# Dealing the projection steps of a two-layer hybrid block by kind of stage

## The chip, the cores and the metric

The kernel runs on one core of one Trainium2 chip. The metric is the device time of one execution in microseconds (us). The core's engines run side by side: TensorE (PE, matrix products), VectorE (DVE), ScalarE (ACT), GpSimd (POOL), and SyncE (SP), which here only issues DMAs.

## The reference

Two layers run over 256 context and 256 latent tokens of width 1024. In each layer one input projection feeds three mixers, and what this change touches is the first two lines and the scan:

```python
att, rw, cv, gt = split(h @ w_in, GROUP_SPLITS)       # h: modulated RMSNorm of the tokens
r, k, v, g, decay, k_dir, kk, a = rwkv_prepare(rw)    # token shift, low-rank decay, norms
# RWKV-7, both directions, 8 heads of 64, context first, then latents from its state:
state = state * w_t + (state @ a_t) b_t^T + v_t k_t^T ;  y_t = state @ r_t
o_rwkv = readout(y, r, k, v, g)                       # group norm, bonus, gate
o_att  = attention(att)                               # 8 query, 2 key heads, rotary
o_conv = b * conv3(c * u)                             # from cv
y = (sum_i sigmoid(gt_i) * (o_i @ w_br_i)) @ w_out    # three branches
x = x + g1 * y ;  x = x + g2 * expert_choice_ffn(...) # 16 experts, latents and context apart
```

In the second layer the context needs only what the latents read of it. Everything is in float32; the projections are split into a high and a low part and take three products.

## The kernel before, in words

Each layer runs in this order: the input norm, a loop over the RWKV scan, attention, the merge of the branches and the output projection (lines 1080 to 1240), and the experts (from line 1290 on), 16 of them with three matrices of 4 MB each to be streamed.

The scan is cut into chunks of 64 tokens and into four groups of two heads, `tau` = 0 to 3. The generator `stages(tau)` yields after each of its stages. Its first 29 are counted by `nx` = 0 to 28: the projections of k, r and v (`shifted`, matmuls into `ps_mm`), decay and step size, the key norm (L479, L484), the decays' scans and the scaled keys (DVE work, L505 to L525), the bonus (L532), the products within a chunk (L552), and the inverse of a unit triangular matrix per chunk. Its 16x16 blocks are inverted by a substitution on DVE (L575, L577); then two rounds of merges join the blocks to 32 and to 64, in the last five of the 29 stages: L591, L595, L609 and L616 are their tiny matmuls, 32x16 or 32x32, and between one and the next ACT and DVE copy, add and transpose (L592 to L619). Four more stages (v transposed at L633, the keys at L645, local products at L657, an empty one) and then eleven follow: the recurrence over eight chunks, with L671, L677 and L685 (`ps_ch`) and short DVE and ACT work in a ring, the output (L703, L707), its group norm (L717 to L729) and its gate (L736). The stages of `tau` + 1 are dealt between the recurrence steps of `tau`, some three at a time.

Filling work comes from the generator `fgen`: the projections of q, k and v of attention, of the convolution, and of 24 branch gates, 360 draws in all (a gate's ninth only closes it), into `ps_mf`. **A step** is one of eight slices of a projection's depth: three matmuls of 512 columns in layer 0 (L116 to L118) and, in layer 1, three of 256 columns (six where the context is needed too; L337). Every fourth step also takes a weight tile: one 256 KB DMA issued on SP (L356), a split into its high part on ACT (L102) and its low part on DVE (L103; three in four or two in three on POOL once attention has begun). After a gate's eighth step come a tanh on ACT (L762) and a DMA on ACT's queue.

`run(g, n, f)` advances a stage generator by n stages and after each of them owes `f` further steps; whole ones are drawn by `fill`. In layer 0 the loop over `tau` is followed by a top-up until 12 of the 24 gates are done (`GB`); in layer 1 the top-up asks for 8, which the loop has passed. The rest is drawn after attention in the text (with some loads of expert weights in between), and the compiler's list scheduler places it among attention's instructions. That scheduler orders each engine's instructions by their place in the text and by when they can be ready, so a step can move ahead of its place, as far as its two `ps_mf` buffers and its weight tiles allow.

Other matmuls in the loop are those of the modulation weights (L200, into `ps_mf` too).

## Time and profile before

| | us |
|---|---|
| median of 3 runs (2316.28 to 2330.32) | 2320.55 |
| profiled execution | 2315.12 |
| its span | 2313.3 |
| busy PE, DVE, ACT, POOL | 2015.0, 990.5, 703.5, 204.0 |
| mean granted TensorE clock | 0.910 of full |

The profiled execution is 1.8 us longer than its span and 5.43 us shorter than the median. Times inside the trace count from the span's start. Layer 0's loop lies from about 45 to 531, its attention to about 640, its experts to about 1269; layer 1's loop from 1278 to 1676, its attention to 1769, its experts from about 1850 to the end. A matmul's duration overlaps the next one's, so the pitch from start to start is what counts in a series of them; a matmul's end is modelled. Granted clock 1.00 is 2.4 GHz, and 0.50 is 1.2 GHz; a mean between them says how much of a stretch ran at which. In a table of stretches the busy times are those of PE, PE's weight loads, DVE, ACT and POOL, and the last three columns are the granted clock, the mean busy share of the 16 DMA engines and GB/s.

### The profile page before, as it was taken

The numbers are of one execution on the slowest core, as the hardware profiler recorded it, in microseconds if no ns is written. First come the engines' busy times: TensorE is split into PE (matmuls) and PEld (weight loads), VectorE is DVE, ScalarE is ACT, GpSimd is POOL, SyncE is SP. The second block draws the span as 40 slices with busy tenths as digits, with TensorE's granted clock in tenths as the row PEclk, the third lists the DMA queues.
The fourth block names the chain that finished last, engine by engine and source line by source line (L and its number), as shares of the span: only waits on it lengthen the run. The fifth ranks groups of instructions, "written<-read, shape, count | busy, mean of one in ns | idle before, by whom it ended". The sixth has DMA issues, their size and how long they took to land.

```text
span 2313.3 us, 44242 instructions
## 1 busy us (share of the span) xinstructions
PE 2015.0 (87%) x18191; PEld 1300.2 (56%) x18191; DVE 990.5 (43%) x2529; ACT 703.5 (30%) x1485; POOL 204.0 (9%) x221
## 2 busy tenths in 40 slices
PE   7999999998999899999987999997878887676765
PEld 3766676676688733333222987886767743232222
DVE  5767667535746511110102759667467511000001
ACT  3443434324523421212002644452354321010001
POOL 1000000003124300000000200000052300000000
PEclk7999999899999999999999989997899997676767
DMA  7333334454278779999999334334376999999997
GB/s 278 111 115 103 119 106 129 126 167 128 60 250 274 256 302 417 419 420 419 420 420 368 93 99 141 111 116 128 117 226 207 305 363 416 416 417 417 417 417 304
DMA packets 340445, 585.08 MB, mean 253 GB/s; under 512 B 20886, under 2 KB 203924, under 8 KB 339988
## 3 DMA queue, kind: packets, MB, share of 16 engines
q1 hardware_dynamic: 326846, 567.76, 67.1%
q10 hardware_dynamic: 13398, 14.50, 1.8%
q8 instruction: 143, 2.34, 0.4%
q14 instruction: 58, 0.48, 0.1%
HBM read 562.79 MB, written 19.40 MB: 252 GB/s over the span
## 4 chain that ended last, share of the span: by engine, by line
PE 41%; DMA 23%; DVE 6%; ACT 2%; issue 2%; POOL 1%; SPq 0%; DVEq 0%; ACTq 0%; POOLq 0%
PE ps_mf L1325 9%; DMA we<-in_exp_down_dram 9%; DMA we<-in_exp_up_dram 6%; DMA we<-in_exp_gate_dram 5%; PE ps_mm L1343 4%; PE ps_mf L337 4%; PE ps_mf L118 2%; PE ps_mf L116 2%; PE ps_mf L117 2%; PE ps_mm L337 2%; PE ps_ch L1167 2%; PE ps_ch L1355 1%; PE ps_sm L552 1%; PE ps_sm L1021 1%; PE ps_sm L1355 1%
## 5 line engine op out<-in xcount | busy, mean ns | idle before, releaser
L1325 PE MATMUL ps_mf<-we,xe 128*32 128x256 f32 (+1 forms) x3040 | 419.2, 534 | 88.0 <-DMA we<-in_exp_up_dram 47.1
L1325 PEld LDWEIGHTS ps_mf<-we,xe 128*32 128x32 f32 (+1 forms) x3040 | 137.2, 134 | 332.8 <-issue 150.2
L1343 PE MATMUL ps_mm<-we,hT 128*32 128x256 f32 (+1 forms) x1536 | 204.3, 526 | 43.2 <-DMA we<-in_exp_down_dram 29.8
L102 ACT ACTIVATE whi<-w 128x512 fp32r<-128x512 f32 x236 | 147.0, 629 | 240.0 <-PE ps_mf L117 73.6
L1330 DVE TENSOR_TENSOR hid<-hid,ps_mf 128x512 f32<-128x512 f32 (+1 forms) x32 | 17.7, 554 | 436.7 <-PE ps_mf L1325 436.0
L103 DVE TENSOR_TENSOR wlo<-w,whi 128x512 fp32r<-128x512 f32 x199 | 137.0, 693 | 81.4 <-ACT whi L102 27.0
L1343 PEld LDWEIGHTS ps_mm<-we,hT 128*32 128x32 f32 (+1 forms) x1536 | 68.4, 133 | 161.7 <-issue 70.7
L337 PE MATMUL ps_mf<-hT,whi 128*128 128x256 f32 x736 | 150.1, 298 | 3.0 <-ACT whi L102 2.8
L116 PE MATMUL ps_mf<-hhi,whi 128*128 128x512 f32 x344 | 143.8, 418 | 1.3 <-ACT csb L779 1.0
L118 PE MATMUL ps_mf<-hhi,wlo 128*128 128x512 f32 x344 | 140.7, 409 | 0.4 <-DVE wlo L103 0.4
L117 PE MATMUL ps_mf<-hlo,whi 128*128 128x512 f32 x344 | 140.4, 408 | 0.0
L1349 DVE TENSOR_TENSOR yg<-ps_mm,g2p 128x512 f32<-128x512 f32 (+1 forms) x32 | 17.9, 558 | 275.2 <-PE ps_mm L1343 275.2
L337 PEld LDWEIGHTS ps_mf<-hT,whi 128*128 128x128 f32 x736 | 117.9, 196 | 14.0 <-issue 4.7
L337 PE MATMUL ps_mf<-hT,wlo 128*128 128x256 f32 x368 | 106.0, 299 | 8.3 <-DVE wlo L103 5.1
L1353 ACT COPY ye<-yg 32x512 f32<-32x512 f32 (+1 forms) x64 | 32.6, 509 | 222.1 <-DVE yg L1349 220.2
L1335 ACT ACTIVATE hT<-ps_sm 128x512 f32<-128x512 f32 (+1 forms) x32 | 15.7, 490 | 235.1 <-PE ps_sm L1334 235.1
L337 PEld LDWEIGHTS ps_mf<-hT,wlo 128*128 128x128 f32 x368 | 70.7, 197 | 14.5 <-DVE wlo L103 5.9
L116 PEld LDWEIGHTS ps_mf<-hhi,whi 128*128 128x128 f32 x344 | 66.0, 192 | 21.4 <-issue 3.9
L118 PEld LDWEIGHTS ps_mf<-hhi,wlo 128*128 128x128 f32 x344 | 66.3, 193 | 16.3 <-issue 1.9
L117 PEld LDWEIGHTS ps_mf<-hlo,whi 128*128 128x128 f32 x344 | 66.1, 192 | 14.7 <-issue 2.6
L337 PE MATMUL ps_mm<-hT,whi 128*128 128x256 f32 x368 | 69.5, 303 | 4.0 <-DVE X L577 2.6
L1173 ACT ACTIVATE xe<-ps_ch,mod,A 128x128 f32<-128x128 f32 x84 | 38.1, 458 | 100.7 <-PE ps_ch L1167 100.6
(476 smaller groups left out, 3775.2 us busy)
## 6 DMA issues: line engine op xcount, KB each, us to landing
we<-in_exp_down_dram SPq DMA_DIRECT2D x124, 1024.0 KB
we<-in_exp_gate_dram SPq DMA_DIRECT2D x118, 1024.0 KB
we<-in_exp_up_dram SPq DMA_DIRECT2D x117, 1024.0 KB
w<-in_w_in_dram SPq DMA_DIRECT2D x228, 256.0 KB
adaw<-in_ada_w_dram SPq DMA_DIRECT2D x160, 256.0 KB
we<-in_exp_gate_dram SPq DMA_DIRECT2D x40, 256.0 KB
adaw<-in_ada_w_dram SPq DMA_DIRECT2D x16, 512.0 KB
cw<-in_w_out_dram SPq DMA_DIRECT2D x32, 256.0 KB
```

Source lines behind the costliest of these rows:

```text
L102: S.activation(hi, src, AF.Copy)
L103: (eng or G).tensor_tensor(lo, src, hi.bitcast(F32), op=ALU.subtract)
L116: P.matmul(o, lh[0], rh[0], start=first, stop=False)
L117: P.matmul(o, lh[0], rh[1], start=False, stop=False)
L118: P.matmul(o, lh[1], rh[0], start=False, stop=last)
L337: P.matmul(o[:, 256 * s - c0:256 * s - c0 + 256], w_[:, j], hT[s][x][:, k], start=first and i == 0 and 256 * s == c0, stop=last and i == 2 ...
L1167: P.matmul(pg, htok[si][:, t, j * 128:(j + 1) * 128], oh[:, t].rearrange("p e c -> p (e c)"), start=(t == 0), stop=(t == 1))
L1173: S.activation(dst, pge, AF.Identity, scale=A2[l][:, j, st_:st_ + 1], bias=mod[l][:, 24 + j, st_:st_ + 1])
L1325: P.matmul(pp[M * g:M * g + M], xe[e // 4][:, j, e % 4], w[:, jj, g * FW:(g + 1) * FW], start=(j == 0), stop=(j == 7), skip_group_check=True)
L1343: P.matmul(pd[M * g:M * g + M], hT2[:, q, M * fg:M * fg + M], w[:, jj, g * FW:(g + 1) * FW], start=(j == 0), stop=(j == 7), skip_group_che ...
L1353: (S.copy, V.tensor_copy)[(g + si) % 2](ye[32 * eg:32 * eg + 32, si, g * FW:(g + 1) * FW], yg[p0:p0 + 32])
L1355: return P.matmul(po, Pw[e // 4][:, tt // 2, (tt % 2) * 128:(tt % 2) * 128 + 128], ye[:, tt // 2, 512 * hf:512 * hf + 512], start=start, s ...
```

## The change

The four numbers per layer in `FR` get new meanings and values. Before, they were steps per stage for `nx` below 12, for the other stages up to 28, for the four stages behind them, and for the eleven of the recurrence and readout (`FL` for `tau` 3). Now they are steps per stage for `nx` below 24, for the merges (`nx` 24 to 28) and the four stages behind them together, for the eleven, and for the eleven of `tau` 3.

```diff
@@ -232,8 +232,7 @@
     SPF = (1, 1)
     SPC = (4, 3)
     GB = (12, 8)
-    FR = ([1.0, 1.0, 1.0, 1.0], [1.2, 1.2, 1.2, 1.2])
-    FL = (1.0, 4.0)
+    FR = ([0.85, 2.0, 1.0, 3.0], [0.95, 3.0, 1.0, 4.0])
     CW = (4, 5)
     CH = (3, 4)
     TH = (2, 3)
@@ -814,22 +813,24 @@
                     fill(f)
                 return True
 
-            FP, FI, FM, FC = FR[l]
+            FP, FM, FC, FL = FR[l]
+            many = lambda nx: FP if nx < 24 else FM
             sg_ = [stages(tau) for tau in range(4)]
             rows1 = vec_rows(1, pw, nc.sync) if l == 0 else None
             run(sg_[0], 12, FP)
             ny = 29
             if l == 0:
                 vec_cols(1, rows1)
-            run(sg_[0], ny - 12, FI)
+            for nx in range(12, ny):
+                run(sg_[0], 1, many(nx))
             for tau in range(4):
                 run(sg_[tau], 4, FM)
                 nx = 0
                 for s in range(11):
-                    run(sg_[tau], 1, FC if tau < 3 else FL[l])
+                    run(sg_[tau], 1, FC if tau < 3 else FL)
                     if tau < 3:
                         for _ in range(ny * min(s + 1, 10) // 10 - nx):
-                            run(sg_[tau + 1], 1, FP if nx < 12 else FI)
+                            run(sg_[tau + 1], 1, many(nx))
                             nx += 1
             while gdone[0] < GB[l] and next(fg, 0) != 0:
                 pass
```

Over a loop, 176 steps become 219.6 in layer 0 and 242 become 276.2 in layer 1. In layer 0 the top-up to 12 gates stays, so the steps done ahead of attention stay the same in number, and it has fewer to do. In layer 1 more steps are done in the loop, and fewer are left for attention.

Three places in PE's order follow. `ps_mf` rows of L116 to L118 or L337 are filling steps; lines of the change are lower by one. First, the merges of `tau` 3 in layer 0, before:

```order
L591 MATMUL ps_sm<-XT,Ad 32x16 x64
L724 MATMUL ps_ch<-ck,yq 128x2 x4
L116 MATMUL ps_mf<-hhi,whi 128x512
L117 MATMUL ps_mf<-hlo,whi 128x512
L595 MATMUL ps_sm<-Xd,Wm 32x16 x64
L118 MATMUL ps_mf<-hhi,wlo 128x512
L729 MATMUL ps_ch<-ck,rq_y 64x128 x8
L116 MATMUL ps_mf<-hhi,whi 128x512
L609 MATMUL ps_sm<-XT,Aa 32x32 x32
```

and now, to the second merge of the same place:

```order
L590 MATMUL ps_sm<-XT,Ad 32x16 x64
L116 MATMUL ps_mf<-hhi,whi 128x512
L117 MATMUL ps_mf<-hlo,whi 128x512
L118 MATMUL ps_mf<-hhi,wlo 128x512
L116 MATMUL ps_mf<-hhi,whi 128x512
L117 MATMUL ps_mf<-hlo,whi 128x512
L118 MATMUL ps_mf<-hhi,wlo 128x512
L716 MATMUL ps_ch<-y,cr 128x512
L594 MATMUL ps_sm<-Xd,Wm 32x16 x64
L723 MATMUL ps_ch<-ck,yq 128x2 x4
```

Between L591 and L595 there were two filling matmuls, and between L595 and L609 two; now there are six ahead of L594 (L595 before), and six follow up to L608.

The same merges in layer 1, before:

```order
L591 MATMUL ps_sm<-XT,Ad 32x16 x64
L729 MATMUL ps_ch<-ck,rq_y 64x128 x4
L595 MATMUL ps_sm<-Xd,Wm 32x16 x64
L736 MATMUL ps_ch<-gl,g2t 128x256
L609 MATMUL ps_sm<-XT,Aa 32x32 x32
L616 MATMUL ps_sm<-Xd,W2T 32x32 x32
```

and now, from L591's place (L590) on:

```order
L590 MATMUL ps_sm<-XT,Ad 32x16 x64
L336 MATMUL ps_mf<-hT,whi 128x256
L336 MATMUL ps_mf<-hT,wlo 128x256
L336 MATMUL ps_mf<-hT,whi 128x256 x2
L594 MATMUL ps_sm<-Xd,Wm 32x16 x64
L728 MATMUL ps_ch<-ck,rq_y 64x128 x4
L735 MATMUL ps_ch<-gl,g2t 128x256
L336 MATMUL ps_mf<-hT,wlo 128x256
L336 MATMUL ps_mf<-hT,whi 128x256 x2
L336 MATMUL ps_mf<-hT,wlo 128x256
L336 MATMUL ps_mf<-hT,whi 128x256 x2
L336 MATMUL ps_mf<-hT,wlo 128x256
```

No filling matmul stood among these merges, and now four stand behind the first and seven ahead of the third.

Last, attention's scores (L1010), transposes (L1021) and products (L1023) in layer 1, before:

```order
L1010 MATMUL ps_ch<-kT,qT 128x512 x2
L337 MATMUL ps_mf<-hT,wlo 128x256
L337 MATMUL ps_mf<-hT,whi 128x256
L1021 MATMUL ps_sm<-ck,pe 128x128 x4
L1010 MATMUL ps_ch<-kT,qT 128x512 x2
L337 MATMUL ps_mf<-hT,whi 128x256
L337 MATMUL ps_mf<-hT,wlo 128x256
L337 MATMUL ps_mf<-hT,whi 128x256 x2
L337 MATMUL ps_mf<-hT,wlo 128x256
L337 MATMUL ps_mf<-hT,whi 128x256 x2
L1021 MATMUL ps_sm<-ck,pe 128x128 x4
```

and now:

```order
L1011 MATMUL ps_ch<-kT,qT 128x512 x6
L1022 MATMUL ps_sm<-ck,pe 128x128 x4
L1011 MATMUL ps_ch<-kT,qT 128x512 x2
L1022 MATMUL ps_sm<-ck,pe 128x128 x4
L1011 MATMUL ps_ch<-kT,qT 128x512 x2
L1022 MATMUL ps_sm<-ck,pe 128x128 x4
L1011 MATMUL ps_ch<-kT,qT 128x512 x2
L1022 MATMUL ps_sm<-ck,pe 128x128 x4
L1011 MATMUL ps_ch<-kT,qT 128x512 x2
L1024 MATMUL ps_mm<-PT,qkv_16919 64x256 x4
L1024 MATMUL ps_mm<-PT,qkv_16920 64x256 x4
```

The filling matmuls, 92 from the first score on, are gone from here.

## Rows read from the trace of the kernel before

**Rows 1.** Page, part 2: the granted clock in 40 slices of 57.8 us.

```profile
PEclk7999999899999999999999989997899997676767
```

**Rows 2.** Stretches of layer 0: length, busy us (instructions) per engine, granted clock, DMA.

```profile
105.00:129.00 24.00, 22.37 (x133) 18.60 (x132) 20.97 (x67) 6.86 (x11) 0.31 (x1) 1.00 0.23 67
149.50:159.70 10.20, 10.20 (x103) 5.74 (x97) 6.46 (x17) 7.92 (x14) 0.00 (x0) 1.00 0.48 140
159.70:213.80 54.10, 49.07 (x498) 33.67 (x496) 44.77 (x134) 15.70 (x32) 1.90 (x6) 0.94 0.48 145
213.80:235.50 21.70, 21.50 (x553) 17.01 (x553) 11.24 (x31) 11.51 (x22) 0.00 (x0) 1.00 0.17 55
264.30:315.50 51.20, 46.05 (x491) 31.84 (x489) 43.75 (x132) 13.23 (x27) 1.89 (x6) 0.93 0.46 140
315.50:337.30 21.80, 21.78 (x554) 17.46 (x554) 12.99 (x34) 12.61 (x24) 0.11 (x1) 1.00 0.14 42
367.20:420.10 52.90, 49.60 (x494) 33.65 (x490) 44.83 (x133) 14.87 (x31) 0.75 (x3) 1.00 0.44 131
420.10:444.60 24.50, 24.22 (x545) 18.52 (x545) 10.17 (x29) 11.27 (x22) 0.00 (x0) 0.79 0.16 49
444.60:488.60 44.00, 39.22 (x470) 24.79 (x470) 19.82 (x67) 6.90 (x16) 0.00 (x0) 0.92 0.52 159
488.60:531.40 42.80, 42.54 (x186) 34.53 (x185) 14.02 (x21) 17.16 (x31) 6.88 (x5) 1.00 0.65 203
```

**Rows 3.** Stretches of layer 1, same columns.

```profile
1356.60:1377.30 20.70, 19.14 (x524) 17.81 (x526) 6.52 (x14) 10.73 (x21) 0.00 (x0) 0.75 0.15 42
1442.50:1462.00 19.50, 17.57 (x534) 16.20 (x536) 8.38 (x19) 9.78 (x19) 0.00 (x0) 0.82 0.25 74
1472.60:1524.20 51.60, 48.94 (x556) 41.87 (x554) 46.44 (x154) 19.50 (x41) 1.89 (x6) 1.00 0.49 145
1524.20:1546.90 22.70, 21.48 (x549) 19.99 (x547) 10.09 (x21) 12.23 (x24) 0.00 (x0) 0.77 0.17 51
1555.60:1610.70 55.10, 45.32 (x464) 36.55 (x465) 41.59 (x134) 16.25 (x36) 0.76 (x3) 0.81 0.48 150
1610.70:1631.80 21.10, 16.99 (x504) 14.95 (x506) 7.12 (x22) 9.12 (x18) 0.00 (x0) 0.60 0.13 38
1675.90:1729.20 53.30, 38.70 (x267) 35.08 (x265) 35.09 (x57) 26.11 (x61) 25.25 (x25) 0.94 0.75 225
1729.20:1768.70 39.50, 34.93 (x254) 28.21 (x252) 29.89 (x75) 22.54 (x54) 8.95 (x7) 1.00 0.60 184
1850.00:1860.00 10.00, 8.26 (x60) 5.47 (x61) 3.58 (x11) 1.72 (x4) 1.54 (x2) 0.63 0.39 130
1860.00:2300.00 440.00, 318.12 (x3222) 128.20 (x3220) 33.29 (x82) 39.66 (x95) 1.23 (x2) 0.73 1.01 412
```

**Rows 4.** Timeline of PE in layer 0: start, duration, engine, instruction, count.

```profile
163.74 0.39 PE L116 MATMUL ps_mf<-hhi,whi 128*128 128x512 f32 x1
163.97 0.40 PE L117 MATMUL ps_mf<-hlo,whi 128*128 128x512 f32 x1
```

**Rows 5.** Timeline of PE in layer 1, same columns.

```profile
1753.24 0.28 PE L337 MATMUL ps_mf<-hT,wlo 128*128 128x256 f32 x1
1753.36 0.40 PE L337 MATMUL ps_mf<-hT,whi 128*128 128x256 f32 x2
```

**Rows 6.** Waits from 1610 to 1632: total us, times, longest.

```profile
PE ps_sm L616 <- DVE W2T L612: 1.5, 1, 1.5
PE ps_sm L609 <- DVE XT L598: 1.2, 1, 1.2
```

**Rows 7.** Page, part 5: the splits' low part: count, busy us, mean ns, idle before.

```profile
L103 DVE TENSOR_TENSOR wlo<-w,whi 128x512 fp32r<-128x512 f32 x199 | 137.0, 693 | 81.4 <-ACT whi L102 27.0
```

**Rows 8.** Groups by line on PE in layer 1's attention, 1729.2 to 1768.7: filling matmuls.

```profile
L337 PE MATMUL ps_mf<-hT,whi 128*128 128x256 f32 x62 | 12.9, 286 | 0.0
L337 PE MATMUL ps_mf<-hT,wlo 128*128 128x256 f32 x32 | 9.2, 288 | 0.3 <-POOL wlo L103 0.3
```

## The prediction

> **What bounds the kernel now.** I read the page's clock line first, then tables of stretches for both loops, then PE's timeline for pitches, and the waits at one place. The clock line [rows 1] is at 9 or more through most of both loops and at 6 to 7 in the last stretch, layer 1's experts. Those run at 412 GB/s with the DMA engines full [rows 3]: they are bound by transfers, and nothing in them changes. Ten microseconds ahead of them the DMA share is only 0.39 [rows 3], so their prefetch is done by then: the stretch starts and ends earlier or later by whatever the loops and attention ahead of it gain or lose.
>
> The two loops have a rhythm. I call the part of a `tau` from its key norm (L479) to the first merge (L591) its **preparation**, from there to its first recurrence matmul its **merges**, and from there to the next key norm its **gap**. In layer 0 the preparations of `tau` 1 to 3 take 54.1, 51.2 and 52.9 us, with DVE busy 44.8, 43.8 and 44.8 and PE 49.1, 46.1 and 49.6 [rows 2]: both are nearly full. The merges take 21.7, 21.8 and 24.5 with PE full and DVE half idle [rows 2]. So steps compete with DVE's share of a preparation, and lengthen merges that PE already fills. Layer 0's loop has little empty PE time: about 5, 5 and 3 us per preparation and 4.8 in `tau` 3's recurrence and readout (44.0 less 39.2) [rows 2]. Layer 1 has more: in `tau` 3's preparation 9.8 us, in its merges 4.1, where two waits for DVE show [rows 3, 6], and a half clock for much of both.
>
> **What moves, and its price.** A filling matmul has a pitch of 0.23 us in layer 0 (163.74 to 163.97) [rows 4] and 0.12 in layer 1 (1753.24 to 1753.36) [rows 5]. I count them by their place in PE's order before and after.
>
> *Layer 0.* 99 leave the top-up behind the loop (182 before, 83 now), which is PE alone, 42.5 of 42.8 us [rows 2]: -22.8 us. They reappear as follows.
> - `tau` 0's preparation has 10 fewer, and DVE is busy 21.0 of its 24.0 us [rows 2]: 0. Two small places, 3 fewer: -0.7.
> - `tau` 0's gap: 28 more, where PE has no hole in 10.2 us [rows 2]: +6.4.
> - `tau` 1's preparation: 4 fewer, -0.9, and some of its 0.06 of missing clock [rows 2], -1.5. `tau` 2's: 1 fewer, -0.2. `tau` 3's: 18 fewer, 4.1 us of PE; DVE's 44.8 of 52.9 [rows 2] lets perhaps half through: -2.0.
> - Merges of `tau` 1 and 2: 27 to 46 and 30 to 49, into a full PE [rows 2]: +4.4 each.
> - Merges of `tau` 3: 21 to 48, +6.2. This stretch ran at a clock of 0.79 with PE busy 24.2 of 24.5 [rows 2]. Taken without its filling it lasts 24.5 - 21 x 0.23 = 19.7 us, against 15.5 and 14.9 for `tau` 1 and 2, whose merges had three to ten filling matmuls between them and a clock of 1.00 [rows 2]. `tau` 3's had two each and now have six; I take 4.5 us off, so +1.7.
> - `tau` 3's recurrence and readout: 49 to 91, +9.6, less its 4.8 of hole and half of the 3.5 missing from its clock of 0.92 [rows 2]: +3.1.
>
> The sum is -8.1.
>
> The clock is where the Trainium skill speaks against the change. The rows: 0.3 us without PE work in `tau` 3's merges and 3.3 in the 52.9 us before them, at 1.00, yet the clock of the merges was 0.79, 10 us at half level [rows 2]. TensorE: Matmul & The Clock Gate (section "Why this matters for your kernels") says that mid-kernel throughput drops come from idle gaps between bursts of matmuls. By that rule filling changes no clock where PE has no hole, the 4.5 us stay, and layer 0's sum would be -3.6; the trace disagrees, since this fall has hardly a hole in it.
>
> *Layer 1.* 92 matmuls leave attention and 4 the stretch before it, 6 come to that stretch, and 90 go into the loop.
> - `tau` 0: preparation +16, of 1.9 us I take +1.0; merges +12, PE has 1.6 us of hole [rows 3] but at other places: +1.4.
> - Three places with 8 fewer together: -1.0. Merges of `tau` 1: 3 more, but 15 now where none stood, and 1.9 us of hole [rows 3]: -1.5.
> - Gaps of `tau` 1 and 2: 25 and 23 more, +3.0 and +2.8. Preparation of `tau` 2: 9 more, +1.1 (DVE 46.4 of 51.6 [rows 3]). Its merges: 11 fewer, none between the first two: -0.5.
> - `tau` 3: preparation 17 fewer, of 2.0 I take 1.0, since its time is neither PE's nor DVE's alone (45.3 and 41.6 of 55.1 [rows 3]); merges 0 to 38, 4.6 us, less 4.1 of hole and 1.5 for a clock of 0.60 [rows 3]: -1.0.
> - Splits: 90 matmuls bring 7.5 tiles, each 0.69 us on DVE [rows 7] (the order has 5 more there and 5 fewer on POOL). Of 5.2 us I take +2.0, since only part falls into preparations. Their DMAs move along on SP, 0.25 MB each, into stretches whose DMA share is about half [rows 2]: 0.
>
> That makes +6.3. In return attention loses 92 of its 94 filling matmuls [rows 8], 11.0 us of PE. It lasts 39.5 us with PE busy 34.9 and DVE 29.9 [rows 3], and of DVE's work only a few splits go with them: at most some -10. But the clock may fall there: layer 1's experts, PE busy 318 of 440, were granted 0.73 [rows 3]. At half clock throughout, PE's remaining 24 us would double to 48: +8.5. I take -5, nearer to DVE's floor, for the experts' clock is a mean of both levels. The stretch before, with 2 more in total, whose time is shared with POOL's 25.2 of 53.3 us [rows 3]: +0.2. The loop's text after attention draws 34 steps fewer and so loads 0.6 MB of expert weights later, hidden behind that 0.39. Layer 1 comes to +1.5.
>
> Both together: -6.6, against the profiled execution's 2315.1 us, so 2308.5. The median of the runs shown lies 5.4 above that execution, so **2314** stands for the median.
>
> **Bounds.** Low: preparations shrink with all their steps (`tau` 0 and 3 of layer 0, -4.4 more), attention at DVE's floor (-5 more), `tau` 3's merges in layer 1 at full clock (0.44 x 16.9 us, below, -6 more): 15 below the forecast, 2299. High is the first rival.
>
> **The rivals.**
> 1. *DVE's floor, slower.* Preparations don't shrink, because DVE sets them; the merges, which the recurrence waits for, grow by all that is put into them. Layer 0: -0.7 + 6.4 + 4.4 + 4.4 + 6.2 + 4.9 - 22.8 = +2.8. Layer 1: 1.9 + 1.4 + 0.4 + 3.0 + 1.1 + 2.8 + 0.5 + 5.2 = +16.3, attention and the stretch before it -4.8: +11.5. Sum +14: **2335**. It decides where `tau` 3's preparation in layer 0 stays above 52 us with 18 matmuls fewer. For it: DVE at 83 to 90 percent there [rows 2, 3]. Against: PE is as full, and DVE's rest of 8 us is no smaller than what is taken. Chance 0.20.
> 2. *Merges warm everywhere, faster.* Layer 1's four merges ran at 0.75, 0.82, 0.77 and 0.60 [rows 3]: twice the missing share times their lengths (20.7, 19.5, 22.7 and 21.1) is 10.3, 7.0, 10.4 and 16.9 us at half level, 44.6 in all. Layer 0's `tau` 3 lost 4.5 in 10.3, 0.44 us per us. 19.6 us, of which the sum holds 1.5: **2296**. Against: in `tau` 0 to 2 of layer 1 the counts hardly rise (30, 30 and 47 to 42, 33 and 36), and merges with as many steps were cold there. Chance 0.13.
> 3. *The clock does not answer to filling.* In the rows: as in layer 1's `tau` 0, cold with 30 matmuls in its merges [rows 3]. Then 4.5 us of layer 0 stay: **2318**. Chance 0.17. It is what the clock page's rule, above, would give.
> 4. *The change hardly does what it says*, since the scheduler places steps by readiness: true of layer 1's `tau` 1 and 2, not of `tau` 3 in either layer. It is in the sum by counts and leaves no case of its own.
>
> **How the numbers follow.** The forecast has 0.50. One per cent, 23 us, is about what a measurement can tell from no change. Only the second rival's lower half and a low end beyond it make it faster than 2297: 0.10. Slower than 2344 needs the first rival and a cold attention (+13.5 to it) at once: 0.05. Within 1%: 0.85. The range of 2296 to 2334 takes in the rivals.
>
> **What would show it.** Layer 0's top-up near 20 us; `tau` 3's merges there about 26 us at a clock near 1.00; its preparation near 51. Layer 1's `tau` 3 merges near 20 us, no hole of over 1 us in them; attention from first score to last product near 34 us. The steps are wrong if attention's scores run at half clock, if the preparations keep their lengths, or if the merges are cold with six matmuls between them.

## The result, and the profile after

The changed kernel takes 2343.53 us (median of 7 runs, 2335.96 to 2352.00) against 2321.66 for the kernel before in the same comparison: a ratio of 1.0094, 95% interval 1.0074 to 1.0114. That is 22 us slower, where 7 us faster was forecast, and above the range. Its profiled execution took 2335.96 us (span 2334.2), against 2315.12 before. The first matmul of layer 1's input norm (L377) starts at 1275.5 instead of 1269.5, and its attention at 1745.6 instead of 1729.2: both layers lose. The clock line of the page answers to [rows 1]:

```profile
PEclk8999999899999899999999999897998997676877
```

It looks the same, and the mean clock is 0.913 after 0.910: the loss is not a slower clock over the whole span. **Half level** below is time at a granted clock of 0.50, worked out from a stretch's mean clock as in the prediction's second rival. Stretches of layer 0 in the changed kernel, with the columns of [rows 2]: `tau` 0's merges and gap, `tau` 1's preparation and merges, `tau` 2's and `tau` 3's preparation and merges, `tau` 3's recurrence and readout, the top-up, and the stretch behind it up to attention's first score.

```profile
128.70:149.60 20.90, 20.21 (x515) 16.66 (x517) 6.66 (x14) 10.69 (x21) 0.00 (x0) 0.76 0.15 41
149.60:166.30 16.70, 16.70 (x131) 11.13 (x128) 10.36 (x23) 9.96 (x17) 0.00 (x0) 1.00 0.47 143
166.30:218.20 51.90, 47.32 (x499) 32.11 (x499) 43.74 (x132) 14.49 (x29) 1.90 (x6) 0.97 0.44 138
218.20:246.60 28.40, 27.91 (x568) 22.00 (x568) 11.73 (x32) 12.85 (x24) 0.00 (x0) 0.88 0.17 52
276.70:329.80 53.10, 45.25 (x477) 31.02 (x473) 43.29 (x130) 13.72 (x27) 1.90 (x6) 0.90 0.39 123
329.80:356.50 26.70, 26.68 (x575) 21.08 (x575) 12.55 (x33) 13.17 (x25) 0.00 (x0) 1.00 0.24 70
386.30:435.70 49.40, 44.44 (x458) 31.04 (x454) 40.57 (x125) 12.40 (x25) 0.75 (x3) 0.90 0.42 130
435.70:465.80 30.10, 29.83 (x575) 22.98 (x574) 11.48 (x31) 13.87 (x26) 0.00 (x0) 0.89 0.21 66
465.80:514.90 49.10, 47.01 (x512) 31.03 (x511) 22.64 (x71) 10.26 (x22) 0.00 (x0) 1.00 0.57 178
514.90:534.70 19.80, 19.80 (x87) 16.02 (x86) 7.08 (x10) 7.28 (x13) 3.64 (x3) 1.00 0.62 203
534.70:575.40 40.70, 30.92 (x147) 24.65 (x145) 25.21 (x42) 19.23 (x41) 15.39 (x14) 0.92 0.47 144
```

The top-up fell by 23 us (42.8 to 19.8), as forecast. The three merges of `tau` 1 to 3 grew by 6.7, 4.9 and 5.6 us; PE had been full there before. The last row is a place that the prediction left out. It now takes 40.7 us with PE busy 30.9. Before, it took 35.5:

```profile
531.40:566.90 35.50, 30.52 (x147) 24.21 (x146) 23.86 (x40) 17.45 (x37) 12.70 (x11) 0.95 0.42 126
```

PE's waits from 534 to 566 in the changed kernel have one large entry (total, times, longest); before, the same wait came to 1.0 us:

```profile
PE ps_sm L937 <- DMA qs<-qkd: 5.8, 1, 5.8
```

L937 transposes the six tiles of q, k and v that attention loads from DRAM (`qkd`), through two buffers. The DMAs issued on SP show where the load of the third tile stood (start, duration, issue):

```profile
517.40 0.34 SPq L737 DMA_DIRECT2D oRd<-y  x1
...
519.81 1.02 SPq L934 DMA_DIRECT2D qs<-qkd  x2
520.88 0.54 SPq L914 DMA_DIRECT2D ob__6918<-oCd  x1
...
533.67 0.32 SPq L914 DMA_DIRECT2D ob__7094<-oRd  x1
...
538.86 0.32 SPq L914 DMA_DIRECT2D ob__7182<-oRd  x1
539.28 0.90 SPq L934 DMA_DIRECT2D qs<-qkd  x2
```

When the loop's last output is stored (`oRd<-y`), SP issues two qkd loads and then eight loads (`ob`) of the convolution's and RWKV's outputs, which the output projection will need. These have two buffers and wait for splits on ACT, DVE and POOL, so the seventh goes out at 538.86, 21 us after that store, and the third qkd load stands behind it. The first transposes had started at 534.7. In the kernel before, SP's eighth `ob` load, PE's first transposes and SP's third qkd load stood like this:

```profile
514.94 0.32 SPq L913 DMA_DIRECT2D ob__7226<-oRd  x1
531.43 1.03 PE L936 MATMUL ps_sm<-ck,qs 128*128 128x128 f32 x8
532.06 0.82 SPq L933 DMA_DIRECT2D qs<-qkd  x2
```

The last `ob` load was out 16 us ahead of the first transpose, and only the transposes were left ahead of the third qkd load.

Layer 1, with the columns of [rows 3]: `tau` 1's merges and gap, `tau` 2's preparation and merges, `tau` 3's preparation, merges, and recurrence with readout, attention from first score to last product, and two pieces of `tau` 2's preparation.

```profile
1446.40:1464.90 18.50, 15.38 (x529) 13.97 (x530) 9.79 (x23) 11.36 (x24) 0.10 (x1) 1.00 0.30 85
1464.90:1478.30 13.40, 13.40 (x139) 10.58 (x136) 7.32 (x19) 9.95 (x17) 0.00 (x0) 1.00 0.40 121
1478.30:1540.00 61.70, 58.02 (x561) 48.59 (x560) 48.39 (x155) 20.79 (x42) 1.79 (x5) 0.86 0.41 120
1540.00:1559.50 19.50, 17.78 (x541) 16.38 (x542) 7.36 (x16) 10.62 (x21) 0.00 (x0) 0.91 0.21 61
1571.00:1626.70 55.70, 44.43 (x445) 35.29 (x446) 40.73 (x128) 15.09 (x34) 0.76 (x3) 0.79 0.44 137
1626.70:1648.40 21.70, 19.30 (x545) 17.46 (x544) 9.12 (x26) 11.48 (x23) 0.00 (x0) 0.84 0.29 85
1648.40:1691.30 42.90, 39.42 (x449) 30.02 (x448) 23.62 (x72) 11.74 (x28) 1.29 (x1) 0.92 0.51 152
1745.60:1787.80 42.20, 31.21 (x160) 19.03 (x160) 27.12 (x73) 16.92 (x41) 0.00 (x0) 0.84 0.40 133
1496.60:1501.00 4.40, 1.95 (x23) 1.52 (x24) 4.40 (x10) 1.67 (x3) 0.44 (x2) 0.97 0.01 4
1501.00:1518.10 17.10, 17.10 (x116) 13.65 (x115) 8.95 (x24) 3.43 (x7) 0.00 (x0) 0.51 0.23 66
```

`tau` 3's merges took their 38 matmuls for 0.6 us more than before [rows 3] in this profile. Attention, which lost 92, did not get shorter: 42.2 us against 39.5. Its groups on PE show why (busy, mean ns, then idle before and what ended it):

```profile
L1011 PE MATMUL ps_ch<-kT,qT 128*128 128x512 f32 x32 | 12.7, 498 | 6.9 <-ACT pe L1017 6.2 <-DVE kT L1002 0.7
L1024 PE MATMUL ps_mm<-PT,qkv 128*64 128x256 f32 x64 | 10.8, 496 | 0.7 <-ACT PT L1023 0.7
L1022 PE MATMUL ps_sm<-ck,pe 128*128 128x128 f32 x64 | 10.3, 306 | 4.1 <-DVE pe L1019 2.7 <-DVE mx L1015 1.2
```

PE stands for 11.7 us where the filling used to be, mostly for ACT's exponentials (L1017) and for DVE's scaling of them (L1019): attention goes round a ring of PE, DVE and ACT. The clock fell besides: 0.84 in this row, 13.7 us at half level, where it was 1.00 with the filling [rows 3].

`tau` 2's preparation took 61.7 us. [rows 3] ends it at 1524.2 before, but the first merge matmul (L591) starts at 1526.1 there, so it had taken 53.5 and is 8 us longer. It has a hole, and behind that 17.1 us at a clock of 0.51. The hole on PE's timeline:

```profile
1499.09 0.70 PE L531 MATMUL ps_sm<-rk,cr 128*128 128x256 f32 x2 [2.45 <-DVE rk L529]
```

### The profile page after: what moved, and what is told of

Same layout as the page of the kernel before. It is cut to its first block, busy times and chain, and to the rows that moved or that the text cites. A ratio compares the mean times of both kernels' runs of the same rounds, so it can differ in the third digit from the quotient of the medians.

```text
span 2334.2 us, 44262 instructions
## 1 busy us (share of the span) xinstructions
PE 2011.1 (86%) x18191; PEld 1296.4 (56%) x18191; DVE 1000.1 (43%) x2534; ACT 704.4 (30%) x1485; POOL 201.3 (9%) x216
## 4 chain that ended last, share of the span: by engine, by line
PE 42%; DMA 21%; DVE 7%; ACT 2%; issue 2%; POOL 1%; SPq 0%; DVEq 0%; ACTq 0%; POOLq 0%
PE ps_mf L1326 9%; DMA we<-in_exp_up_dram 8%; DMA we<-in_exp_down_dram 8%; PE ps_mf L336 5%; PE ps_mm L1344 4%; DMA we<-in_exp_gate_dram 4%; PE ps_mf L116 3%; PE ps_mf L118 3%; PE ps_mf L117 2%; PE ps_mm L336 2%; PE ps_ch L1168 2%; PE ps_sm L551 1%; PE ps_mm L1024 1%; PE ps_ch L1356 1%; PE ps_sm L1022 1%
## 5 line engine op out<-in xcount | busy, mean ns | idle before, releaser
L1326 PE MATMUL ps_mf<-we,xe 128*32 128x256 f32 (+1 forms) x3040 | 411.6, 522 | 93.3 <-DMA we<-in_exp_up_dram 52.2
L102 ACT ACTIVATE whi<-w 128x512 fp32r<-128x512 f32 x236 | 147.4, 629 | 255.5 <-PE ps_mf L336 83.8
L103 DVE TENSOR_TENSOR wlo<-w,whi 128x512 fp32r<-128x512 f32 x204 | 141.8, 698 | 101.3 <-PE ps_mm L118 31.3
L336 PE MATMUL ps_mf<-hT,whi 128*128 128x256 f32 x736 | 156.0, 307 | 4.2 <-ACT whi L102 3.3
L116 PE MATMUL ps_mf<-hhi,whi 128*128 128x512 f32 x344 | 146.3, 425 | 1.2 <-ACT th L761 1.0
L118 PE MATMUL ps_mf<-hhi,wlo 128*128 128x512 f32 x344 | 138.5, 402 | 0.0
L336 PEld LDWEIGHTS ps_mf<-hT,whi 128*128 128x128 f32 x736 | 121.3, 203 | 19.2 <-issue 8.4
L336 PE MATMUL ps_mf<-hT,wlo 128*128 128x256 f32 x368 | 108.7, 306 | 6.9 <-DVE wlo L103 5.5
L1354 ACT COPY ye<-yg 32x512 f32<-32x512 f32 (+1 forms) x64 | 32.6, 509 | 226.5 <-DVE yg L1350 224.6
L336 PEld LDWEIGHTS ps_mf<-hT,wlo 128*128 128x128 f32 x368 | 73.1, 203 | 11.8 <-DVE wlo L103 7.5
L116 PEld LDWEIGHTS ps_mf<-hhi,whi 128*128 128x128 f32 x344 | 65.4, 190 | 21.4 <-issue 6.3
L118 PEld LDWEIGHTS ps_mf<-hhi,wlo 128*128 128x128 f32 x344 | 65.6, 191 | 15.1 <-issue 2.2
L336 PE MATMUL ps_mm<-hT,whi 128*128 128x256 f32 x368 | 66.5, 291 | 0.8 <-DVE gl L414 0.4
```

Of the source, the lines that this page charges most:

```text
L102: S.activation(hi, src, AF.Copy)
L103: (eng or G).tensor_tensor(lo, src, hi.bitcast(F32), op=ALU.subtract)
L116: P.matmul(o, lh[0], rh[0], start=first, stop=False)
L118: P.matmul(o, lh[1], rh[0], start=False, stop=last)
L336: P.matmul(o[:, 256 * s - c0:256 * s - c0 + 256], w_[:, j], hT[s][x][:, k], start=first and i == 0 and 256 * s == c0, stop=last and i == 2 ...
L1326: P.matmul(pp[M * g:M * g + M], xe[e // 4][:, j, e % 4], w[:, jj, g * FW:(g + 1) * FW], start=(j == 0), stop=(j == 7), skip_group_check=True)
```

## The experiments

All were timed in five rounds beside the kernel before, whose median lay between 2320.3 and 2324.0 us; ratios are to it. The edits are to the changed kernel. `[1.0, 1.0, 1.0, 1.0]` and `[1.2, 1.2, 1.2, 4.0]` in `FR` give the dealing of before in layer 0 and layer 1. Lengths of stretches are from one profile of each kernel.

**One layer at a time.**

```diff
-    FR = ([0.85, 2.0, 1.0, 3.0], [0.95, 3.0, 1.0, 4.0])
+    FR = ([0.85, 2.0, 1.0, 3.0], [1.2, 1.2, 1.2, 4.0])   # e1: layer 0's part alone
+    FR = ([1.0, 1.0, 1.0, 1.0], [0.95, 3.0, 1.0, 4.0])   # e2: layer 1's part alone
```

> The new dealing in layer 0 alone, layer 1 as before. My theory (exposed filling): most of the loss is layer 1's, where filling that was free inside attention now stands in the loop; the two profiles differ by only 6 us at the start of layer 1. It expects about 2327, +6. Rival (DVE's floor in both layers): layer 0 has 99 matmuls of 0.23 us in its merges, recurrence and first gap that its preparations don't give back, so it carries at least half of the 22 us: 2332 or more.

Measured: 2330.41 us, 1.0045 (1.0026 to 1.0064), some 10 us slower: between the two theories' numbers.

> The new dealing in layer 1 alone, layer 0 as before. Exposed filling: +15, 2336: the loop grows by about 11 us for 90 matmuls of 0.12 us, and attention, bare, takes 42 us and not 39.5. DVE's floor in both layers: +10 or less, 2331.

Measured: 2334.97 us, 1.0059 (1.0037 to 1.0080). Both layers lose, about 10 and 14 us, and the two add up to the whole within their intervals.

**Is filling worth anything to attention in layer 1?** e3 is the change, but puts filling back into attention by taking it from `tau` 3's recurrence; e4 has the dealing of before, but empties attention into that recurrence.

```diff
+    FR = ([0.85, 2.0, 1.0, 3.0], [0.95, 3.0, 1.0, 0.89])   # e3
+    FR = ([1.0, 1.0, 1.0, 1.0], [1.2, 1.2, 1.2, 7.1])   # e4
```

> The changed kernel, but in layer 1 tau 3's recurrence is dealt 0.89 steps per stage and not 4, so that the loop draws as many steps in all as before (242), and 53 filling matmuls stand in attention again; layer 1's preparations and merges stay as in the change. Exposed filling: the 60 matmuls leave a recurrence with hardly a hole (-7 us) and attention is back near 39.5 (-3): about 2333, 10 below the change. Rival (the half-clock stretches in the preparations of tau 2 and 3 in layer 1 make the loss): within 4 us of the change, 2340 or more.

Measured: 2349.75 us, 1.0118 (1.0090 to 1.0145): no better than the change, and 17 us above what the theory had. Up to its first output matmul, `tau` 3's recurrence with 27 filling matmuls took 33.3 us, no less than with 84 (32.6 before), and 21.7 us of it were at half level. Filling that is taken out gives nothing back there either.

> The kernel before, but tau 3's recurrence in layer 1 is dealt 7.1 steps per stage and not 4: 34 steps more in the loop, as in the change, all behind the merges, and no filling matmul left in attention. Preparations and merges are as before. Exposed filling: the recurrence grows by 80 matmuls of 0.12 us less some 4 us of hole, +6, and attention takes 42 us, +3: about 2330. Rival (attention does give the time back, as I forecast, and the loss lies in how the loop is dealt): attention near 34, the total at 2321 or below.

Measured: 2330.53 us, 1.0037 (1.0020 to 1.0055). The recurrence took 37.9 us with 150 filling matmuls; 66 more cost 5.2 us. Attention, emptied, took 41.9:

```profile
1737.10:1779.00 41.90, 30.04 (x160) 17.70 (x160) 27.25 (x73) 17.17 (x44) 1.29 (x1) 0.88 0.39 134
```

Over all the runs told here, attention from first score to last product lasted 39.2 to 41.1 us in the ten profiles with 92 filling matmuls in it (mean 40.2), 39.8 and 41.0 in two with 89, 40.2 in one with 115, 41.9 in one with 53, and 40.0 to 42.3 in the six with none (mean 41.2). It gives nothing back for its filling. Part of that is the clock: bare attention spent 6.8 to 15.0 us at half level in its six profiles, and attention with 92 filling matmuls 0 to 8.2 in its ten. But the two bare ones with the least of it (6.8 us) still took 40.0 and 40.1 us, against 39.2 to 39.5 in the four filled ones with none.

**Layer 0's part in two, and a dose.** The tail is `tau` 3's recurrence and readout. The runs are the dense tail alone (e5), the thin preparations and dense merges alone (e6), and a denser tail (e7).

```diff
+    FR = ([1.0, 1.0, 1.0, 3.0], [1.2, 1.2, 1.2, 4.0])   # e5
+    FR = ([0.85, 2.0, 1.0, 1.0], [1.2, 1.2, 1.2, 4.0])   # e6
+    FR = ([1.0, 1.0, 1.0, 5.0], [1.2, 1.2, 1.2, 4.0])   # e7
```

> Dealing of before everywhere, but layer 0's last recurrence (tau 3, eleven stages) gets three steps per stage in place of one: 93 filling matmuls in its recurrence and readout where 49 stood, 138 in the top-up where 182 stood. Theory 'place' (filling is free only where PE waits, and the top-up is cover for attention's loading until it is shorter than about 26 us): top-up -10 us to about 32, so no wait for the load of qkd; recurrence and readout +5 as in the run of layer 0's part alone; sum -5, about 2316, ratio 0.998. Theory 'clock' (any denser dealing brings new half-clock stretches, which eat what is saved): recurrence and readout no shorter in sum, 2321 to 2326. Rival 'the tail is the loss' (tau 3's recurrence takes its filling at full pitch, 0.23 us): +10 and -10, 2321.

Measured: 2315.85 us, 0.9976 (0.9956 to 0.9995), some 6 us faster, as the first theory had it in sum. One step of it failed: with a top-up of 32.3 us PE still waited 4.3 us for the third qkd load, so a cover of 26 us was not enough.

> The other half of layer 0's part: 0.85 steps per stage ahead of the merges, two in the merges, and the last recurrence as before (one per stage); layer 1 as before. Top-up 119 matmuls, about 27 us, so by the theory 'place' the load of qkd is nearly covered (wait under 1 us). Theory 'place': the merges of tau 1 to 3 +6.6, +5 to +7 and +3 to +5, the gap of tau 0 +6.5, preparations -2 to -5 in all, top-up -15: sum about +6 to +10, 2327 to 2331, that is, all of what layer 0's part loses without its wait. Theory 'wait' (layer 0's loss is the uncovered load of qkd alone): within 3 us of before, 2321.

Measured: 2329.06 us, 1.0026 (1.0002 to 1.0049). The merges of `tau` 1 to 3 took 28.1, 30.2 and 28.7 us, and the gap 16.7. This half loses some 6 us by itself (0.5 to 11, which does not quite exclude the second theory's 3), and the wait for qkd, 3.4 us, is the smaller part of it. This profile's mean clock was 0.872, the lowest of all, so its lengths are upper ones.

The two halves don't add up: 6 us faster and 6 us slower by themselves, and 10 slower together (e1). The stretches behind the loop show a reason. From e6 to e1 the dense tail is added while the top-up is short already: recurrence and readout take 5.4 us more, the top-up 8.2 less, and the stretch from the first transpose to the first score 4.8 more, 2.0 us lost in sum. Under the long top-up the same tail (e5 against the mean of the six profiles with layer 0's dealing and buffers of before) gives +4.7, -11.3 and +4.3, 2.3 us gained. A shorter top-up is worth less the more of its cover is gone.

> As the run with three steps per stage in layer 0's last recurrence, but five: 141 matmuls in recurrence and readout, 90 in the top-up, about 21 us. Theory 'place' with the load of qkd landing some 26 us after the loop: PE waits about 5 us for it at attention's first score; of the 21 us taken from the top-up, 17 or more come back in the recurrence (48 more at the full pitch of 0.23 beyond the holes), so 2321 to 2328, slower than three per stage. If the load is issued earlier when the loop is longer (its issue follows the loop's text and not the top-up's length), no wait shows, and the time is 2316 to 2321.

Measured: 2326.38 us, 1.0015 (0.9994 to 1.0036). Recurrence and readout took 61.5 us in place of 44.0, 17.5 more: 92 more matmuls at 0.23 are 21.2 us, less 4.8 of hole 16.4. PE waited 8.8 us for qkd.

**What did the long top-up cover?** First six buffers in place of two, so that no qkd load waits for a transpose (attention's score tiles share these buffers); once with the change, once with the dealing of before, once with the dense tail.

```diff
-    QB = (2, 2)
+    QB = (6, 2)   # e9; e10 and e11 with FR of before and of e5
```

> The change as it is, but attention in layer 0 loads its six qkd tiles into six buffers instead of two, so that SP issues all six loads right after the store of o_rwkv and ahead of the eight loads for the output projection, with no wait for a transpose. 18 filling matmuls move from the stretch between the first transpose and the first score product into attention. Theory 'uncovered load' (the 5.8 us in which PE waits for the third load cost what they show): the wait goes, the time falls by 4 to 6 us against the change, ratio to before about 1.007 in place of 1.0094. Theory 'it only moves' (attention in layer 0 is held by its ring, and starts earlier for nothing): 1.009 again.

Measured: 2342.01 us, 1.0078 (1.0056 to 1.0101), which excludes neither theory's ratio. The six loads went out at 523.67, ahead of the eight, and yet the stretch from the first transpose to the first score took 35.8 us, 4.9 less, with 18 filling matmuls fewer (4.1 us). PE's wait there, and ACT's ahead of it:

```profile
PE ps_sm L937 <- ACT qkv L940: 4.7, 1, 4.7
```

```profile
ACT ohC L102 <- DMA ob__6918<-oCd: 4.6, 1, 4.6
ACT ohC L102 <- DMA ob__7006<-oCd: 3.0, 1, 3.0
```

The wait only changed its name. ACT copies half of the transposed tiles (`qkv`, L940). On its timeline four splits (L102) of `ob` tiles stand ahead of these copies and two more between them, waiting for their loads.

> The dealing of before in both layers, with the six buffers for the qkd loads: the control for the run of the change with six buffers and for the two below. With the top-up of 182 matmuls PE waited 1.0 us for those loads, so theory 'uncovered load' expects -1 us, within 2 us of before: 0.998 to 1.000. If the buffers help in another place (attention's score tiles share them), it would be faster here by more than 2 us, and the gain in the other run is not the load's.

Measured: 2316.39 us, 0.9982 (0.9963 to 1.0001): up to 9 us faster, so this control doesn't exclude a gain of the buffers by themselves of the size seen with the change.

> Dealing of before but for three steps per stage in layer 0's last recurrence (the run at 0.9976), with six buffers. There PE waited 4.3 us for the third qkd load. Theory 'uncovered load': 3 to 4 us better than that run, about 2312 against 2321 to 2323, ratio 0.995 to 0.997. Theory 'it only moves': 0.9976 again.

Measured: 2318.27 us, 0.9983 (0.9966 to 0.9999), no better than without the buffers; PE waited 4.1 us for ACT. Then the eight loads were put behind attention, into eight buffers of a pool of their own:

```diff
-    QB = (2, 2)
+    QB = (6, 2)
...
-                    ob_ = po.tile([128, NW], F32, name="ob_", bufs=OBB[l])
+                    ob_ = po.tile([128, NW], F32, name="ob_", bufs=2) if lat else pb_.tile([128, NW], F32, name="ob_", bufs=8)
...
         obs = obg()
+        ebo = ExitStack()
+        pb_ = ebo.enter_context(pool(f"ob{l}"))
```

> The change, with six buffers for the qkd loads and with the eight loads of the convolution's and RWKV's outputs for the output projection (L914, and their splits on ACT, DVE and POOL) moved behind attention, into buffers of their own. Theory 'eight loads' (what the top-up of 20 us no longer covers is the chain of these loads and splits): no wait of over 2 us between the first transpose and attention's first score; the stretch from the first transpose to it loses 4 to 6 us against the run of the change with six buffers, ratio to before 1.005 to 1.006. They may cost up to 5 us at the output projection, where their splits are then due: the control below shows it. Theory 'attention starts when it can anyway': 1.008 again.

Measured: 2335.88 us, 1.0051 (1.0034 to 1.0069), as the theory had it, though its interval overlaps that of e9; the stretches tell more. From the first transpose to the first score, with six buffers alone (e9):

```profile
538.60:574.40 35.80, 27.41 (x129) 22.42 (x127) 24.42 (x42) 19.96 (x42) 15.27 (x14) 0.90 0.42 129
```

and with the eight loads behind attention (e13), with the same 129 instructions on PE:

```profile
538.60:567.60 29.00, 25.77 (x129) 21.22 (x127) 21.46 (x38) 15.83 (x33) 11.13 (x10) 0.94 0.34 101
```

It is 6.8 us shorter, and DVE, ACT and POOL have 4, 9 and 4 instructions fewer, of which 4, 8 and 4 are the splits of the eight tiles. This is what the long top-up had covered.

> The dealing of before in both layers with six buffers and the eight loads behind attention: the control. Under its top-up of 43 us these loads were hidden, so moving them gains nothing ahead of attention (0 to -2 us, as with the buffers alone: 0.998) and may cost up to 5 us at the output projection, where their splits are due at once: 0.998 to 1.001.

Measured: 2321.95 us, 0.9986 (0.9969 to 1.0004). Under the long top-up moving the loads changes nothing that can be told from none, and the stretch from the first transpose to the first score takes 29.0 us with the loads ahead of attention (e10) and 28.9 with them behind it (e15).

> Three steps per stage in layer 0's last recurrence alone, with six buffers and the eight loads behind attention. Theory 'eight loads': no wait between the top-up and attention's first score, 4 us better than with six buffers alone: about 2314 to 2315 against before's 2321 to 2322, ratio 0.996 to 0.997; 3 to 5 us better than the control below. Rival 'nothing to gain': 0.998 as with the buffers alone, and no better than the control.

Measured: 2314.03 us, 0.9951 (0.9931 to 0.9971), the lowest ratio here, ahead of both kernels; its interval just meets the control's. Recurrence and readout, top-up, and the stretch behind it, in the control (e15):

```profile
449.30:495.60 46.30, 40.59 (x470) 25.73 (x470) 19.76 (x67) 6.89 (x16) 0.00 (x0) 0.89 0.49 150
495.60:537.90 42.30, 42.30 (x187) 34.63 (x186) 11.80 (x17) 12.97 (x23) 1.29 (x1) 1.00 0.58 182
537.90:566.80 28.90, 24.19 (x129) 19.67 (x127) 21.93 (x38) 15.78 (x33) 11.13 (x10) 1.00 0.35 101
```

and with three steps per stage in the recurrence (e14):

```profile
444.10:493.60 49.50, 48.22 (x515) 31.34 (x514) 22.55 (x71) 10.38 (x22) 0.00 (x0) 1.00 0.54 166
493.60:525.80 32.20, 32.20 (x142) 26.30 (x141) 9.12 (x13) 9.40 (x16) 1.29 (x1) 1.00 0.63 199
525.80:555.50 29.70, 26.75 (x130) 22.35 (x129) 22.06 (x38) 15.86 (x33) 11.14 (x10) 0.89 0.32 92
```

The top-up gives 10.1 us, the recurrence takes 3.2 of them for 44 more matmuls (10.1 us at their pitch), and 0.8 are lost behind it.

> As the run at 0.9951 (three steps per stage in layer 0's last recurrence, six buffers, eight loads behind attention), but two steps per stage: 69 filling matmuls in recurrence and readout where there were 49 and 93, 162 in the top-up where there were 182 and 138. Theory 'holes': the recurrence's 4.7 us of hole take some 20 matmuls for nothing, so top-up -4.6, recurrence +0 to +1: 3.5 to 4.6 us better than the control at 0.9986, about 0.997. Theory 'all of the gain is the clock of the recurrence' (three steps kept it at full level, one did not): between the two, with the recurrence's clock deciding.

The edit is `FR = ([1.0, 1.0, 1.0, 2.0], ...)`. Measured: 2313.88 us, 0.9969 (0.9950 to 0.9988). Recurrence and readout took 45.1 us, 1.2 less than in the control with 20 matmuls more; the top-up took 37.7. The sum is as the theory 'holes' had it, but the recurrence was at full clock here and not in the control, so this run does not part the two theories.

**Layer 1: what makes the loop longer?** Dense merges for `tau` 3 alone, with 1.1 steps per stage elsewhere (e8, and e12 with the dense tail and six buffers), dense merges without thin preparations (e17), and thin preparations without dense merges, with 1.0 in the recurrence of `tau` 0 to 2 (e16).

```diff
+    FR = ([1.0, 1.0, 1.0, 1.0], [1.1, 3.0, 1.1, 4.0])   # e8; e12 has 3.0 as layer 0's last, and QB = (6, 2)
+            many = lambda nx, t=0: FM if nx >= 24 and t >= 3 * l else FP
...
+    FR = ([1.0, 1.0, 1.0, 1.0], [0.95, 1.2, 1.0, 4.0])   # e16
+    FR = ([1.0, 1.0, 1.0, 1.0], [1.2, 3.0, 1.2, 4.0])   # e17
```

> Layer 0 as before. In layer 1 three steps per stage only in the merges of tau 3 (and the four stages behind them), 1.1 per stage in place of 1.2 elsewhere, so that attention keeps its filling (89 to 94 matmuls, as before): 41 matmuls in tau 3's merges where none stood, 37 fewer in the preparations of tau 1 to 3, 10 fewer in tau 2's merges. Theory 'place': the merges of tau 3 keep their 21 us (their 4 us of holes and the half clock take the filling), and the preparations and merges that lose 47 matmuls get 3 to 5 us shorter: 2316 to 2318. Theory 'DVE's floor': preparations keep their lengths, merges +0 to +5: 2321 to 2326. Theory 'clock': a new half-clock stretch in one of the preparations, as tau 2's in the run of layer 1's part alone, +3 to +8: 2324 to 2329.

Measured: 2322.28 us, 0.9988 (0.9967 to 1.0008): no gain that can be told. `tau` 3's merges took 22.5 us with 41 matmuls (21.1 with none), but `tau` 2's preparation and merges took 4.0 us more with 24 fewer.

> All that helped at once: three steps per stage in layer 0's last recurrence, six buffers, and in layer 1 three per stage in tau 3's merges alone with 1.1 elsewhere. Theory 'place': the parts add, 0.996 of the run above and -1 to -3 us for layer 1: about 2310, ratio 0.994 to 0.996. Theory 'clock' (layer 1's part was nothing but chance): the same as the run above, within 1 us.

Measured: 2320.95 us, 0.9995 (0.9975 to 1.0014). The parts don't add; `tau` 2's preparation took 61.7 us, 17.1 of them at half level.

> Layer 0 as before. Layer 1 with three steps per stage in the merges and the four stages behind them and 1.2 elsewhere, as before: dense merges without thin preparations. Gaps of tau 0 to 2 have 64, 80 and 59 filling matmuls where 42, 33 and 18 stood, at 0.12 us each: 2.6 + 5.6 + 4.9 = +13 us, and attention's filling is gone, which gives nothing back (theory 'place'): +13 to +17, 2334 to 2338. If half-clock stretches follow thin preparations, none is new in tau 1's merges or tau 2's preparation here, and the time stays at the lower end; if they follow dense merges and gaps, both are cold again as in the change (+8), 2342. If attention did give back its filling (11 us), 2325.

Measured: 2344.74 us, 1.0080 (1.0048 to 1.0112). The three gaps grew by 12.7 us, at the pitch of L336's matmuls: 110 more, 26 of them filling and 84 the scan's own projections (`ps_mm`), which the filling had pushed out of the places ahead. Attention, without any filling, took 42.3. `tau` 1's preparation, whose filling was as before, took 62.5 us, with 20.4 at half level.

> Layer 0 as before. Layer 1 with 0.95 steps per stage ahead of the merges and 1.2 in the merges and behind them, as before, and 1.0 in the recurrence of tau 0 to 2: thin preparations without dense merges, and 62 more branch matmuls left for attention. PE's order has 28 fewer filling matmuls in tau 1's preparation, 59 fewer in tau 2's, 42 fewer in tau 0's gap and 48 more in tau 2's. Theory 'place': gaps -5 + 5.8, preparations -3 to -7 in sum, attention +0 to +7 for 69 more: within 4 us of before, 2320 to 2328. If half-clock stretches follow thin preparations, tau 1's merges or tau 2's preparation is at half level for some 17 us as in the change, and it is 5 to 10 us slower, 2329 to 2334.

Measured: 2329.19 us, 1.0035 (1.0012 to 1.0057). `tau` 1's preparation took 60.9 us with 28 matmuls of L336 fewer (15.0 at half level) and `tau` 2's 55.5 with 59 fewer (13.6 at half level). In these two profiles either edit brings half level to the middle of the loop. With layer 1's dealing of before (e4's but for its last number among them), one of eleven profiles has over 10 us of it in `tau` 1's preparation, its merges or `tau` 2's preparation; with any other, eight of nine have. Which property of the order brings it stays open: ahead of it stood a hole of 2.45 us in the change, of 1.85 in e12 and of 1.49 in e17, but in e2, e3 and e13 none over 0.5 us in the ten before the fall in `tau` 1's merges.

## Why the prediction was wrong

Since many runs share one layer's dealing, a stretch can be averaged over profiles: for layer 0's loop 14 with the dealing of before and 6 with the new one (recurrence and top-up without those whose tail differs), for layer 1 11 and 5. Microseconds against before, the main places:

| | forecast | measured |
|---|---|---|
| layer 0: gap of `tau` 0 | +6.4 | +6.5 |
| preparations of `tau` 1, 2, 3 | -2.4, -0.2, -2.0 | -1.5, +2.4, -4.4 |
| merges of `tau` 1, 2, 3 | +4.4, +4.4, +1.7 | +5.8, +7.0, +5.3 |
| `tau` 3's recurrence and readout | +3.1 | +3.9 |
| top-up | -22.8 | -23.6 |
| top-up to attention's first score | 0 | +5.2 (after - before) |
| layer 1: gaps of `tau` 1, 2 | +3.0, +2.8 | +2.8, +2.8 |
| merges of `tau` 1, 3 | -1.5, -1.0 | +4.2, +2.1 |
| preparations of `tau` 2, 3 | +1.1, -1.0 | +4.0, -1.5 |
| attention (0 against 92 filling matmuls) | -5 | +1.0 |

In sum, layer 0 was forecast at -8.1 us and cost about 10 by itself (e1); layer 1 was forecast at +1.5 and cost about 14 (e2).

**Right.** The two pitches, the gaps, the top-up, `tau` 3's recurrence in both layers, and that `tau` 3's preparation in layer 0 shrinks when steps leave it: it is 49.4 us, so the first rival's sign (above 52) was not met, though its 2335 is the nearest of the times.

**Right in sum, wrong in name.** The counts at L116 to L118 and L337 take in the scan's own projections of k, r and v (`ps_mm`), which are no filling. Of the 28 more in layer 0's gap of `tau` 0, 12 are filling; of the 25 in layer 1's gap of `tau` 1, 3 are. In layer 1's merges of `tau` 1, 30 matmuls of own projections became 22 filling and 9 own, and the others slid into the gap (18 to 40). Filling that is dealt to a full place pushes other work on, and that work costs the same pitch. The bound at 1524.2 [rows 3] also put 11 of `tau` 2's matmuls into its merges: with the bound at 1526.1 its preparation has 2 fewer (not 9 more) and its merges as many as before (not 11 fewer).

**Wrong, and why.** Four steps failed.
- *Attention gives back 5 us for its 92 matmuls.* It gives none. I went by PE's busy time, 34.9 of 39.5, and by DVE's; neither sets the time. PE's waits in the ring through DVE and ACT do (11.7 us of them in the changed kernel), and the colder clock adds to them. Zero lay between my ends (-10 and +8.5), and I went half way to DVE's floor without asking what PE would wait for in the filling's place. The sign that I named, scores at half clock, was met in part (13.7 of 42.2 us).
- *Behind the top-up nothing changes.* The top-up was 42.8 us of pure filling, but it covered eight loads, their splits, and through ACT's queue the copies of q, k and v. Of the 23 us gained, 5.2 were lost again there in the change, and 6.8 was what the eight loads cost once the buffers were added (e9 against e13). I asked what bounds the top-up and not what runs beneath it.
- *Merges of `tau` 1 and 2 at +4.4 each, and full clock for `tau` 3's merges in layer 0, worth 4.5 us.* Taken without its filling, `tau` 3's stretch is 23.8 - 21 x 0.23 = 19.0 us before and 29.1 - 48 x 0.23 = 18.1 after: 0.9 us, so the third rival was right there. `tau` 1's merges took 28.1 to 28.5 us in all six profiles, at 0.88 in the one shown, where they had run at 1.00 [rows 2] and taken 21.6 to 22.3 in eleven of fourteen. So the clock fell in merges that had been warm, which no term of the sum allowed for.
- *Layer 1's loop costs 6.3 us.* Its gaps cost what was reckoned; on top came half level, over 10 us of it in `tau` 1's merges or `tau` 2's preparation in all five profiles, and these two places grew by 8 us together. For the loop the prediction had a price for cold merges getting warmer, and none for a warm place getting cold.

On the clock the Trainium skill (TensorE: Matmul & The Clock Gate, "Why this matters for your kernels") names idle gaps between bursts of matmuls. The 2.45 us hole ahead of the 0.51 is such a gap, but no run shows that it brought the fall, and e2, e3 and e13 fell without one; `tau` 1's merges in layer 0, PE busy 27.9 of 28.4 us at 0.88, disagree.

Taken together: filling costs nothing in layer 1's attention, where PE waits in a ring, less than its pitch in `tau` 3's recurrence (44 matmuls for 3.2 us of 10.1 in e14) and in layer 1's merges of `tau` 3 (38 for 2.1 us of 4.6), and its pitch or more where PE is full (layer 0's gap of `tau` 0 and its merges of `tau` 1 and 2). In layer 1 the change moved it from the first of these to the others. In layer 0 it moved it out of a place that is full but covers loads. The one part that moved it well, `tau` 3's recurrence in layer 0, gives the lowest ratio by itself once the loads are out of the way. Not settled is what brings the half level; the two places where it appeared hold 8 us of layer 1's 14, and it has some of layer 0's merges.

## What to carry to other kernels

Before filler work is moved, ask of the place it leaves whether it runs in another engine's waits (then little or nothing comes back) and what loads and queues it covers (then part of the gain is lost again), and of the place it goes to how much of PE's time there is empty: busy shares of one engine don't answer the first, the waits of a run without the filler do. A wait removed by buffers can come back under another engine's name when a shared queue stands behind the same loads; follow it once more before calling it gone.

## What the runs showed of the hardware

- Denser filling went with a higher clock in `tau` 3's recurrence and readout of layer 0. With the dealing of before it spent 0 to 17.1 us at half level in eight profiles (none in one of them, 6.8 in the kernel before); with two to five steps per stage, none in eleven of eleven, as in the rows of e14 above (1.00 against 0.89).
- Layer 1's recurrence of `tau` 3, up to its first output matmul, shows the same over a wider dose: 21.7 us at half level with 27 filling matmuls (e3), 17.1 with 72 (e17), 13.7 with 75 (e16), 0 to 6.8 in fourteen profiles with 84, and none with 87 (e8, e12) and 150 (e4).
- In the tiny matmuls of layer 0's merges the same did not hold. With the new dealing `tau` 1's merges had 6.8 us at half level in the change, though PE had no hole over 0.8 us there; with that of before eleven of fourteen profiles had none. No run parts the dense merges from the thin preparations ahead of them in layer 0.
- A busy PE did not bring the clock back in `tau` 2's preparation of the changed kernel: it was busy in all of the 17.1 us at 0.51 (1501.0 to 1518.1).
